# A hybrid decoder layer: the low parts of 28 weight splits made by VectorE instead of GpSimd

## The chip, the core and the metric

The kernel runs on one core of one Trainium2 chip. The core has five engines, each with its own in-order queue of instructions: TensorE (PE in the profile, with its weight loads as PEld), VectorE (DVE), ScalarE (ACT), GpSimd (POOL) and SyncE (SP, which here only starts transfers). The engines wait for one another on semaphores. The metric is the device time of one execution in microseconds (us), the median of the runs shown; lower is better.

## The reference

One decoder layer in float32 over a sequence of 2048 tokens and a model width of 1024. Two groups of heads work side by side on the same normed input, their outputs are concatenated and go through one output projection, and a SwiGLU feed-forward network follows. Cut to what matters here:

```python
hn = rms_norm(h, mix_pre_g)
proj = hn @ w_in
...
attn_out = sliding_window_attention(q, k, v, attn_sinks, rel_bias)
conv_out = conformer_conv(u, conv_dw, conv_dw_b, conv_ln_g, conv_ln_b, w_conv_pw)
mixed = jnp.concatenate([attn_out, conv_out], axis=-1) @ w_out
h = h + rms_norm(mixed, mix_post_g)
hn = rms_norm(h, ffn_pre_g)
ff = (jax.nn.silu(hn @ w_gate) * (hn @ w_up)) @ w_down
h = h + rms_norm(ff, ffn_post_g)
```

The last step of `conformer_conv` is a pointwise product with `w_conv_pw` (512 x 512) with nothing between it and the lower half of `w_out`. The two matrices can therefore be multiplied with each other once, ahead of the data.

## The kernel before

**Products in three parts.** TensorE multiplies in a reduced format (fp32r). To keep the precision of float32, each operand is split into a high part, which is the value rounded to fp32r, and a low part, raw − high, and a product is made of three matmuls: high·high, high·low and low·high (`three`). For the weights the split is made in `split_w`: ScalarE copies the raw tile into the high half (line 133), then the subtraction raw − high makes the low half. The subtraction runs either on GpSimd (`ptt`, line 135 in the trace) or on VectorE (`vtt`, which goes through the wrapper `dve` and is seen as line 85). A tile of 128 x 512 is split at a time. If a place in DRAM is given (`low`), the low half is also stored there (line 137), so that later token blocks load it (line 132) instead of making it again. `weight` loads a raw tile of two blocks and splits both.

**Stages.** The 2048 tokens are worked in four blocks of 512, t = 0 to 3:

- A0 to A3: the input projection, 14 units of 24 matmuls for each block (`mm@A` in the profile). The low parts of the weights of the first six units of block 0 are made on GpSimd, the others on VectorE.
- B0 to B3: attention of a block, in steps for each 128 queries. TensorE makes the scores (`tr@B<-kz,ql@A`), VectorE masks them (`COPY_PREDICATED`, line 457), adds the bias and takes the maximum (line 460), and prepares the shift (`sm@B`); ScalarE takes the exponentials (line 479); VectorE sums, takes the reciprocal and scales the probabilities (`p@B<-p@B,sm@B`); TensorE transposes them (line 501), ScalarE copies them out (line 502), GpSimd masks a copy (`AFFINE_SELECT`, line 504), and TensorE multiplies with the values.
- C0 to C3: the convolution over time, 480 instructions `fc@C` on VectorE (taps), followed by the normalisation over channels. The taps are put behind other work by a lower priority and, in `dve`, by an order tie to the last other VectorE instruction.
- J (`stage_join`): the product of `w_conv_pw` with the lower half of `w_out`, made once. Four raw tiles of `w_out` give eight splits (the right operands, in buffers `mid` and `chl`), two raw tiles of `w_conv_pw` give four (the left operands, in `yt`); the raw tiles lie in `wx` and `mb`. The result goes through `ct@J` and `fa@J` to DRAM as `w_join`.
- W0 to W3 (`stage_w`): the output projection of a block with norm and residual. Only W0 makes low parts of its weights (eight raw tiles, 16 splits, the first half of them of `w_out` and the second of `w_join`) and stores them in `lo_out`; W1 to W3 load them.
- H, F and G: the feed-forward network (gate and up, then down), in which VectorE makes the low parts of its operands as well (`w@F<-chl@F,w@F`).

**What sets the order.** The stages are generators on lanes that are advanced by credits: J runs on a lane beside A2 and A3, W0 beside A3 and the attention of block 2, so that their few instructions lie between those of the projection. Within that, the order of each engine's queue is not written out by hand: the tile framework places the instructions of each engine by priorities and by a simulated time line of the whole program. A change of one instruction's engine can therefore change the order of others, on all engines. Dependencies through tiles become semaphore waits.

**Buffers.** All tiles of a name share a fixed number of buffers: 6 for `w`, 2 for `raw`, 1 for `wx`, 2 for `mb`, 4 for `mid`, 5 for `chl`, 1 for `yt`. The banks of PSUM are 3 for `tr`, 4 for `mm` and 1 for `ct`. A load into a buffer waits for the last reader of what lay there.

Of the kernel before, what the change touches and what calls it, by code (L numbers as in the profile page):

```python
# [12 lines left out]
F32 = mybir.dt.float32  # L13
# [12 lines left out]
P = 128  # L26
# [11 lines left out]
def layer_kernel(ctx, tc, x, xT, cols, rows, sinks, relb, onehot, w_in, w_pw, w_out, w_gate, w_up, w_down, out):  # L38
    nc = tc.nc
# [7 lines left out]
    lab = ["X0"]  # L47
# [7 lines left out]
    def t_(tag, shape, dt=F32):  # L55
        return sb.tile(list(shape), dt, tag=tag, name=nm(tag), bufs=BUFS[tag])

    def f4(tag, shape=(P, D)):
        return t_(tag, shape)

    def f2(tag, shape=(P, T)):
        return t_(tag, shape)

    def hl(tag):
        return t_(tag, (P, 2, T), F32R)
# [63 lines left out]
    def split_w(raw, tag, low=None, made=False, on_pool=True):  # L129
        w = tag if not isinstance(tag, str) else hl(tag)  # L130
        if made:
            nc.sync.dma_start(w[:, 1].bitcast(F32), low)
        act(w[:, 0], raw, AF.Copy)  # L133
        if not made:
            (ptt if on_pool else vtt)(w[:, 1], raw, w[:, 0].bitcast(F32), ALU.subtract)
            if low is not None:
                (nc.gpsimd if on_pool else nc.sync).dma_start(low, w[:, 1].bitcast(F32))
        return w

    def weight(src, low, made, raw=None, on_pool=True):  # L140
        if raw is None:
            raw = t_("raw", (P, 2, T))
            nc.sync.dma_start(raw, src)
        return [split_w(raw[:, n], "w", low[n], made, on_pool) for n in range(2)]
# [43 lines left out]
    def three(o, pairs, first=True, last=True):  # L188
        n = 3 * len(pairs)
        i = 0  # L190
        for (sh, sl), (mh, ml) in pairs:
            for a, b in ((sh, mh), (sh, ml), (sl, mh)):
                mat(o, a, b, start=first and i == 0, stop=last and i == n - 1)
                i += 1

    lo_in = dr.tile([2 * KC - 2, 2, P, T], F32, name="lo_in")
    lo_out = dr.tile([2, KC, P, T], F32, name="lo_out")
# [425 lines left out]
    def spare_tile():  # L623
        if not spare:
            spare.append(t_("mb", (P, 2, T)))
        return spare[0]

    def stage_join():
        lab[0] = "J0"
        srcs = [w_out[4 + k].rearrange("p (a b) -> p a b", a=2) for k in range(4)]  # L630
        srcs += [w_pw[2 * m : 2 * m + 2].rearrange("m p t -> p m t") for m in range(2)]
        raws = {}

        def load(i):
            if i < len(srcs):
                lab[0] = "J0"
                raws[i] = spare_tile() if i % 2 else f4("wx", (P, 2, T))
                nc.sync.dma_start(raws[i], srcs[i])

        load(0)  # L640
        load(1)
        yield JL
        right = []
        for k in range(4):
            for n in range(2):
                lab[0] = "J0"
                right.append(split_w(raws[k][:, n], "mid" if k < 2 else "chl"))
            yield JS
            load(k + 2)
            yield JS  # L650
        for mp in range(2):
            lab[0] = "J0"
            pair_ = t_("yt", (P, 2, 2, T), F32R)
            left = [split_w(raws[4 + mp][:, m], pair_[:, m]).rearrange("p a (k c) -> p a k c", c=P) for m in range(2)]
            yield 2
            for m in range(2):
                for n in range(2):
                    lab[0] = "J0"
                    o = ct()
                    three(o, [((left[m][:, 0, k], left[m][:, 1, k]), (right[2 * k + n][:, 0], right[2 * k + n][:, 1])) for k in range(4)])  # L660
                    z = f2("fa")
                    act(z, o, AF.Copy, scale=0.5)
                    nc.scalar.dma_start(w_join[2 * mp + m, :, n * T : (n + 1) * T], z)
                    yield 4
                    lab[0] = "J0"
# [37 lines left out]
    def block_half(acc, units, n, first, L, bank_of, s0=0):  # L703
        cs = slice(n * T, (n + 1) * T)
        for i in range(len(acc)):
            s = i + s0
            lab[0] = L
            o = bank_of()
            three(o, [((a[s // 4][:, 0, ss(s)], a[s // 4][:, 1, ss(s)]), (w[:, 0], w[:, 1])) for a, w in units])
            if first:  # L710
                act(acc[i][:, cs], o, AF.Copy)
            else:
                vtt(acc[i][:, cs], acc[i][:, cs], o, ALU.add)
            yield 0.65 * len(units)

    def load_gb(row):
        gb = []
        for n in range(2):
            t = f2("gb")
            nc.sync.dma_start(t, rows[row, n * T : (n + 1) * T].partition_broadcast(P))  # L720
            gb.append(t)
        return gb
# [6 lines left out]
    def stage_w(w, spill, G, atag, htag, mtag, bank_of, norm=None):  # L729
        L = f"W{w}"  # L730
        lab[0] = L
        acc = [f4(atag) for _ in range(4)]

        def acts(gi, ms=None):
            aa = []
            for m in ms or load(gi):
                a = hl(htag)
                act(a[:, 0], m, AF.Copy)
                vtt(a[:, 1], m, a[:, 0].bitcast(F32), ALU.subtract)
                aa.append([a])  # L740
            return aa

        stage = spare_tile() if w == 1 else None

        def load(gi):
            ms = []
            for c in range(G * gi, G * gi + G):
                ms.append(stage[:, c % 2] if w == 1 else f2(mtag))
                nc.sync.dma_start(ms[-1], mixT[c, :, w * T : (w + 1) * T])
            return ms  # L750

        first = load(0)
        gb = load_gb(0) if w > 1 else None
        if w != 1:
            yield 5.0 if w == 0 else 8.0
            lab[0] = L
        nxt = acts(0, first)
        for gi in range(KC // G):
            aa = nxt
            for n in range(2):  # L760
                lab[0] = L
                if n == 0 and gi + 1 < KC // G:
                    if w < 2 and G * gi + G == 4:
                        ld.until(f"C{w}")
                        lab[0] = L
                    rows_next = load(gi + 1)
                if n == 1 and gi + 1 < KC // G:
                    nxt = acts(gi + 1, rows_next)
                src = w_out[2 * gi : 2 * gi + 2] if gi < 2 else w_join[2 * gi - 4 : 2 * gi - 2]
                ws = weight(src[:, :, n * T : (n + 1) * T].rearrange("c p t -> p c t"),  # L770
                            lo_out[n, 2 * gi : 2 * gi + 2], w > 0)
                yield from block_half(acc, list(zip(aa, ws)), n, gi == 0, L, bank_of)
        tail = norm_w(w, spill, acc, mtag, gb)
        if norm:
            norm(tail)
        else:
            yield from tail
# [627 lines left out]

    lb.add("X", stage_x(), lambda: "x1" in started)
    lw.add("W0", stage_w(0, True, 2, "x", "hl", "fa", mm), lambda: "A3" in started and "J" in ld.done)
    TGA = [["hl"] * 8, ["mid"] * 4 + ["chl"] * 4, ["hl"] * 8, ["mid"] * 4 + ["hl"] * 4]
    xa = {}
# [4 lines left out]
    for t in range(NT):  # L1414
        lc.add(f"T{t}", stage_taps(t))
    ld.add("J", stage_join(), lambda: "A2" in started)
    for t in range(2):
        ld.add(f"C{t}", stage_tail(t), lambda t=t: since(lc, f"T{t}", CS))
# [40 lines left out]
    for n, off in (("B11", 0), ("B21", 4)):  # L1459
        lh.add(n + ".0", stage_h_plain(ws, ops, n, off), lambda: since(lw, "W0", NH))  # L1460
    run(stage_w(1, True, 2, "mid", "hl", "at", mm, norm=lambda g: lh.add("N1", g)))
    lc.hold = lambda: "S0" not in lh.done
    lh.add("S0", stage_h_sums(ws, ops), lambda: f"P0.{PRE_S0}" in started and "B3" in lb.done)
# [6 lines left out]
    ws, ops = (2, 3), {}  # L1470
    lw.add("C2", stage_tail(2))
    lw.add("W2", stage_w(2, True, 2, "mid", "ql", "at", tr))
    lw.add("C3", stage_tail(3), lambda: since(lc, "T3", CS))
    lw.add("W3", stage_w(3, True, 2, "mid", "ql", "at", tr, norm=lambda g: lw.add("N3", g)))
# [72 lines left out]
```

## Time and profile before

| | before |
|---|---|
| runs, us | 1981.5, 1977.93, 1981.22 |
| median, us | 1981.22 |
| profiled execution, us | 1986.73 |
| its span, us | 1984.7 |
| mean granted clock of TensorE in it | 0.992 |

The profile is of one execution, and its times count from the start of the span. An instruction is named by line, engine, operation, and by the tiles that it writes and reads (`out<-in`), without their numbers; `x` counts instructions. In the timelines instructions of one kind that follow each other are joined in one row, with the time of the row; what stands in brackets is the idle time of that engine just before, and the instruction (or transfer) whose end released it. A granted clock of 1.00 is full speed of TensorE. The joining lies at about 185 to 300 us of the span, the making of low parts in W0 at about 330 to 443 us, the down-projection of the first half begins near 1000 us.

### The profile page before, as it was taken

The page shows a single profiled execution, that of the slowest core. Times are in us where ns is not written, and L with a number is a line of the kernel's source. Part 1 is how long each engine was busy: PE and PEld are TensorE (multiplying, and loading weights), DVE is VectorE, ACT ScalarE, POOL GpSimd, SP SyncE. Part 2 cuts the span into 40 slices and gives each one's busy share as a digit, 9 for nine tenths or more (in the row PEclk, how much of TensorE's full clock was granted, in tenths as well). Part 3 has the DMA queues.
Part 4 walks back from the last instruction along what each step waited for, and adds up shares of the span by engine and source line. Part 5 has one row for each costly group of instructions (what it writes and reads, how often), then busy time and mean ns, then how long its engine had stood idle before and what let it go on. Part 6 is the DMA issues. An engine that isn't in the chain of part 4 may idle for free.

```text
span 1984.7 us, 26851 instructions
## 1 busy us (share of the span) xinstructions
PE 1937.4 (98%) x8730; PEld 1545.6 (78%) x8730; DVE 1493.7 (75%) x2679; ACT 969.5 (49%) x1910; POOL 335.2 (17%) x395
## 2 busy tenths in 40 slices
PE   9999999999999999989999999999999999999998
PEld 7877667677768878768878878777888888888886
DVE  5998989697793899888748995688766665455557
ACT  5455334546576633333345446477544433345443
POOL 6001212331120300000000011005423332311000
PEclk9999999999999999999999999999999999999999
DMA  8886646568758676686577778679745442366654
GB/s 313 275 308 224 203 149 186 181 193 305 270 166 303 224 252 223 230 275 233 193 241 252 226 270 276 215 291 345 265 142 176 170 153 91 136 224 202 212 190 155
DMA packets 229181, 443.56 MB, mean 223 GB/s; under 512 B 22920, under 2 KB 48688, under 8 KB 229040
## 3 DMA queue, kind: packets, MB, share of 16 engines
q1 hardware_dynamic: 207408, 406.19, 61.0%
q10 hardware_dynamic: 19392, 28.32, 3.9%
q0 software_dynamic: 2240, 7.34, 0.9%
q8 instruction: 68, 1.11, 0.2%
q14 instruction: 73, 0.60, 0.1%
HBM read 320.64 MB, written 121.12 MB: 223 GB/s over the span
## 4 chain that ended last, share of the span: by engine, by line
PE 77%; DVE 8%; DMA 8%; ACT 3%; issue 2%; POOL 1%; SPq 0%; ACTq 0%; DVEq 0%; POOLq 0%
PE mm@F L108 36%; PE mm@G L108 16%; PE mm@A L108 12%; PE mm@W L108 4%; PE tr@W L108 3%; PE tr@B L108 3%; DVE fc@C L85 3%; PE ct@J L108 1%; DMA raw@A<-w_in 1%; DVE mid@W L85 1%; DMA at@W<-mixT 1%; DMA gb@F<-keeps 1%; DMA mids<-fa@F 1%; DVE w@F L85 1%; DMA mixT<-fc@C 1%
## 5 line engine op out<-in xcount | busy, mean ns | idle before, releaser
L85 DVE SCALAR_TENSOR_TENSOR fc@C<-glu@C,colt,fc@C 128x512 f32<-128x512 f32 x480 | 365.9, 778 | 2.2
L108 PE MATMUL mm@F<-hl@H,w@F 128*128 128x512 f32 x1056 | 257.6, 392 | 3.5 <-ACT mm@F L983 3.5
L108 PEld LDWEIGHTS mm@F<-hl@H,w@F 128*128 128x128 f32 x1056 | 198.7, 189 | 48.4 <-ACT mm@F L983 4.8
L108 PE MATMUL mm@G<-hl@G,hl@G 128*128 128x512 f32 x924 | 226.0, 395 | 6.6 <-ACT mm@G L1249 2.2
L108 PE MATMUL mm@A<-hl@A,w@A 128*128 128x512 f32 x840 | 209.3, 399 | 2.1 <-DVE hl@A L85 1.1
L108 PEld LDWEIGHTS mm@G<-hl@G,hl@G 128*128 128x128 f32 x924 | 172.3, 189 | 45.5 <-ACT mm@G L1249 2.6
L108 PE MATMUL mm@G<-w@G,hl@G 128*128 128x512 f32 x876 | 199.5, 389 | 0.0
L829 ACT ACTIVATE w@F<-chl@F 128x512 fp32r<-128x512 f32 x220 | 134.7, 624 | 126.4 <-PE mm@F L108 119.3
L108 PEld LDWEIGHTS mm@G<-w@G,hl@G 128*128 128x128 f32 x876 | 164.4, 188 | 34.1
L108 PEld LDWEIGHTS mm@A<-hl@A,w@A 128*128 128x128 f32 x840 | 156.8, 190 | 40.6 <-issue 3.6
L85 DVE TENSOR_TENSOR w@F<-chl@F,w@F 128x512 fp32r<-128x512 f32 x198 | 143.3, 728 | 36.9 <-ACT w@F L829 36.4
L108 PE MATMUL mm@F<-ql@H,w@F 128*128 128x512 f32 x528 | 131.3, 392 | 7.2 <-ACT mm@F L1071 3.7
L108 PE MATMUL mm@F<-mid@H,w@F 128*128 128x512 f32 x528 | 131.3, 391 | 2.8 <-ACT fa@F L1092 2.6
L108 PE MATMUL mm@F<-p@H,w@F 128*128 128x512 f32 x528 | 131.2, 394 | 0.0
L108 PE MATMUL mm@F<-x@H,w@F 128*128 128x512 f32 x528 | 127.5, 390 | 0.0
L108 PEld LDWEIGHTS mm@F<-ql@H,w@F 128*128 128x128 f32 x528 | 98.6, 188 | 28.6 <-ACT mm@F L1071 4.6
L108 PEld LDWEIGHTS mm@F<-mid@H,w@F 128*128 128x128 f32 x528 | 98.6, 188 | 24.9 <-ACT fa@F L1092 3.5
L108 PEld LDWEIGHTS mm@F<-p@H,w@F 128*128 128x128 f32 x528 | 100.7, 191 | 21.6 <-ACT at@F L1085 0.3
L108 PEld LDWEIGHTS mm@F<-x@H,w@F 128*128 128x128 f32 x528 | 98.6, 188 | 21.3 <-DVE sm@B L460 0.8
L133 ACT ACTIVATE w@A<-raw@A 128x512 fp32r<-128x512 f32 x110 | 67.4, 626 | 77.4 <-PE mm@A L108 42.9
L108 PE MATMUL mm@W<-w@W,hl@W 128*128 128x512 f32 x384 | 103.2, 408 | 1.6 <-ACT fa@A L355 1.6
L85 DVE TENSOR_TENSOR w@G<-raw@G,w@G 128x512 fp32r<-128x512 f32 x73 | 51.5, 705 | 67.7 <-ACT w@G L829 66.7
(308 smaller groups left out, 3313.9 us busy)
## 6 DMA issues: line engine op xcount, KB each, us to landing
mids<-fa@F SPq DMA_DIRECT2D x154, 256.0 KB, 2.8
raw@A<-w_in SPq DMA_DIRECT2D x55, 512.0 KB, 4.7
w@A<-lo_in SPq DMA_DIRECT2D x84, 256.0 KB, 3.7
fc@G<-mids SPq DMA_DIRECT2D x77, 256.0 KB, 3.3
fa@G<-mids SPq DMA_DIRECT2D x75, 256.0 KB, 5.0
w@W<-lo_out SPq DMA_DIRECT2D x48, 256.0 KB, 4.1
chl@F<-w_gate SPq DMA_DIRECT2D x22, 512.0 KB, 4.2
raw@F<-w_gate SPq DMA_DIRECT2D x22, 512.0 KB, 3.7
```

What stands on the lines that cost most here:

```text
L85: r = op(*args, **kw)
L108: r = nc.tensor.matmul(*args, **kw)
L133: act(w[:, 0], raw, AF.Copy)
L829: act(w[:, 0], x, AF.Copy)
```

## The change

Four lines. `split_w` has an argument `on_pool`, true by default, that picks the engine of the subtraction. The change passes `on_pool=False` at the two calls in `stage_join` (12 subtractions of 128 x 512) and in `stage_w` (16 in W0; the later blocks make none). The store of a low part, which used to go with the engine of the subtraction, is kept on GpSimd's queue for the W stages.

```diff
         if not made:
             (ptt if on_pool else vtt)(w[:, 1], raw, w[:, 0].bitcast(F32), ALU.subtract)
             if low is not None:
-                (nc.gpsimd if on_pool else nc.sync).dma_start(low, w[:, 1].bitcast(F32))
+                (nc.gpsimd if on_pool or lab[0][0] == "W" else nc.sync).dma_start(low, w[:, 1].bitcast(F32))
         return w
...
-                right.append(split_w(raws[k][:, n], "mid" if k < 2 else "chl"))
+                right.append(split_w(raws[k][:, n], "mid" if k < 2 else "chl", on_pool=False))
...
-            left = [split_w(raws[4 + mp][:, m], pair_[:, m]).rearrange("p a (k c) -> p a k c", c=P) for m in range(2)]
+            left = [split_w(raws[4 + mp][:, m], pair_[:, m], on_pool=False).rearrange("p a (k c) -> p a k c", c=P) for m in range(2)]
...
                 ws = weight(src[:, :, n * T : (n + 1) * T].rearrange("c p t -> p c t"),
-                            lo_out[n, 2 * gi : 2 * gi + 2], w > 0)
+                            lo_out[n, 2 * gi : 2 * gi + 2], w > 0, on_pool=False)
```

In the built program 28 instructions of line 135 leave GpSimd's queue and stand as subtractions of line 85 in VectorE's; the 16 stores of `lo_out` (line 137) stay on GpSimd's queue and now wait for VectorE. Counted from the start, VectorE's queue is the same up to the row that the trace shows at 192 us. From there to the beginning of the down-projection the order of the queues of all engines differs in places, and behind it it is the same again.

## The prediction

> **What bounds the kernel now.** I read the page first: busy times and the chain that ended last.
>
> ```profile
> span 1984.7 us, 26851 instructions
> PE 1937.4 (98%) x8730; PEld 1545.6 (78%) x8730; DVE 1493.7 (75%) x2679; ACT 969.5 (49%) x1910; POOL 335.2 (17%) x395
> PE 77%; DVE 8%; DMA 8%; ACT 3%; issue 2%; POOL 1%; SPq 0%; ACTq 0%; DVEq 0%; POOLq 0%
> ```
>
> TensorE (PE) bounds the whole: 1984.7 − 1937.4 = 47 us is all that it doesn't work. The change gives it no less to do, so it can gain only where PE stands still or runs at a lower clock beside the 28 subtractions that move. The next view is the busy time in stretches of 20 us over the two places (start and end, length, then busy time and count of PE, weight load, DVE, ACT, POOL, then clock, DMA share, GB/s).
>
> ```profile
> 180.00:200.00 20.00, 19.84 (x99) 15.01 (x98) 15.37 (x32) 11.03 (x32) 8.78 (x7) 1.00 0.79 287
> 200.00:220.00 20.00, 17.77 (x87) 12.01 (x83) 20.00 (x22) 8.76 (x17) 11.71 (x8) 1.00 0.73 249
> 220.00:240.00 20.00, 17.96 (x79) 13.97 (x80) 19.75 (x53) 7.24 (x24) 0.00 (x0) 0.83 0.47 151
> 360.00:380.00 20.00, 18.04 (x93) 13.97 (x90) 15.54 (x45) 19.89 (x57) 7.12 (x9) 1.00 0.51 162
> 380.00:400.00 20.00, 20.00 (x70) 10.96 (x69) 11.99 (x27) 6.41 (x11) 3.07 (x4) 1.00 0.57 176
> ```
>
> In the joining (about 185 to 225 us) DVE is full, PE falls to 17.8 of 20, and the clock drops after it. In the first output projection (332 to 442 us) DVE has room and the clock is full. The timeline of PE between 203 and 233 us shows what it waits for (start, time, instruction and count; in brackets the idle time ahead and its releaser), and two windows of 10 us show the clock.
>
> ```profile
> 205.10 0.66 PE L501 MATMUL tr@B<-ident,p@B 128*128 128x128 f32 x4 [1.12 <-DVE p@B L85]
> 206.87 0.63 PE L501 MATMUL tr@B<-ident,p@B 128*128 128x128 f32 x4 [1.11 <-DVE p@B L85]
> ...
> 215.58 4.42 PE L108 MATMUL mm@A<-hl@A,w@A 128*128 128x512 f32 x18
> ...
> 225.76 1.86 PE L108 MATMUL tr@B<-kz,ql@A 64*128 64x256 f32 x12 [2.04 <-DVE sm@B L460]
> 227.55 5.76 PE L108 MATMUL mm@A<-hl@A,w@A 128*128 128x512 f32 x14
> ```
>
> ```profile
> 220.00:230.00 10.00, 7.96 (x33) 6.12 (x34) 9.86 (x26) 1.68 (x3) 0.00 (x0) 0.78 0.55 186
> 230.00:240.00 10.00, 10.00 (x48) 7.86 (x47) 9.89 (x28) 5.56 (x21) 0.00 (x0) 0.88 0.40 117
> ```
>
> Three PE gaps, 1.12 + 1.11 + 2.04 = 4.3 us, all end on DVE. Behind the third the clock falls: 10 × (1 − 0.78) + 10 × (1 − 0.88) = 3.4 us lost (matmuls take 5.76/14 = 0.41 us against 4.42/18 = 0.25 us). So 7.7 us hang on DVE's lateness there.
>
> **Why DVE is late.** The timeline of DVE, then that of POOL, over the same stretch:
>
> ```profile
> 162.83 1.28 DVE L85 TENSOR_TENSOR p@B<-p@B,sm@B 128x512 f32<-128x512 f32 x2
> 173.52 1.88 DVE L85 TENSOR_TENSOR hl@A<-x@A,hl@A 128x512 fp32r<-128x512 f32 x3
> ...
> 193.11 1.25 DVE L85 SCALAR_TENSOR_TENSOR sm@B<-sm@B,nsnk 128x8 f32<-128x8 f32 x1
> 200.55 2.82 DVE L85 SCALAR_TENSOR_TENSOR fc@C<-glu@C,colt,fc@C 128x512 f32<-128x512 f32 x2
> 203.28 3.44 DVE L85 TENSOR_TENSOR p@B<-p@B,sm@B 128x512 f32<-128x512 f32 x2
> 206.65 10.18 DVE L85 SCALAR_TENSOR_TENSOR fc@C<-glu@C,colt,fc@C 128x512 f32<-128x512 f32 x11
> 217.36 4.05 DVE L85 SCALAR_TENSOR_TENSOR fc@C<-glu@C,colt,fc@C 128x512 f32<-128x512 f32 x6
> 223.66 0.74 DVE L457 COPY_PREDICATED tr@B<-upper,tr@B 128x256 f32<-128x256 int8 x2
> ```
>
> ```profile
> 187.84 3.54 POOL L135 TENSOR_TENSOR mid@J<-wx@J,mid@J 128x512 fp32r<-128x512 f32 x2 [0.65 <-ACT mid@J L133]
> 202.78 3.40 POOL L135 TENSOR_TENSOR chl@J<-mb@J,chl@J 128x512 fp32r<-128x512 f32 x2
> 207.45 3.46 POOL L135 TENSOR_TENSOR yt@J<-wx@J,yt@J 128x512 fp32r<-128x512 f32 x2 [1.27 <-ACT yt@J L133]
> ```
>
> DVE instructions that read two operands stretch where POOL's subtractions run: the two p@B multiplies take 3.44 us at 203 against 1.28 us at 163, two conv taps 2.82 us at 200 against 4.05/6 × 2 = 1.35 us at 217. POOL's own take 1.7 us each.
>
> **The change part by part: the joining.** Ten subtractions come to DVE in this stretch (eight right, two left). The same subtraction on DVE, hl@A, takes 1.88/3 = 0.63 us, so +6.2 us. What falls away, from the groups of DVE instructions of 180 to 225 us, and after it of 226 to 270 us, where POOL runs no such work (count, busy us, mean ns, idle before):
>
> ```profile
> L85 DVE SCALAR_TENSOR_TENSOR fc@C<-glu@C,colt,fc@C 128x512 f32<-128x512 f32 x35 | 30.1, 898 | 0.2
> L85 DVE TENSOR_TENSOR p@B<-p@B,sm@B 128x512 f32<-128x512 f32 x2 | 3.4, 1760 | 0.0
> ...
> L85 DVE SCALAR_TENSOR_TENSOR fc@C<-glu@C,colt,fc@C 128x512 f32<-128x512 f32 x38 | 27.7, 754 | 0.4
> L85 DVE TENSOR_TENSOR p@B<-p@B,sm@B 128x512 f32<-128x512 f32 x4 | 2.6, 680 | 0.0
> ```
>
> 35 × (0.898 − 0.754) + 2 × (1.76 − 0.68) = 7.2 us. DVE's total thus stays about level (−1 us); what counts is the order. In the built program of the changed kernel the eight right subtractions stand ahead of the p@B multiplies, with one tap fewer; the two multiplies end, counted from 192.2 us in undisturbed durations, at about 204.7 and 205.3 us. PE has 14 projection matmuls more ahead of the transposes that read them, 14 × 0.25 = 3.5 us of cover: it comes to them at about 207. Both first gaps go: −2.2 us.
>
> Next late is the bank of the scores, which the copy of 223.66 and four reductions free. Between the multiplies and that copy stand 16 taps (19 before), two subtractions, the rest as before: 16 × 0.67 + 2 × 0.63 + 1.7 = 13.7 us, so the copy starts near 219 and the banks are free near 222. PE has 18 matmuls more ahead of its next transposes into them (+4.5 us, less the 2.2 us it gained) and asks for them near 226. Slack 4 us: the third gap goes (−2.0), and the clock with it (−3.4). The bounds: nothing, if raws come late (SyncE's loads of wx and mb now wait for DVE's reads instead of POOL's, some 3 us later for the first); −7.7 with all. I take −7.7, as 4 us of slack stand against these 3.
>
> **The first output projection.** Sixteen subtractions leave POOL; their DMAs stay on its queue.
>
> ```profile
> L135 POOL TENSOR_TENSOR w@W<-raw@W,w@W x16: 1262/1296/2571, 331.5 to 440.6; 128x512 fp32r<-128x512 f32 x16
>   ACT w@W L133: 46.0, 8
> L137 POOL DMA_DIRECT2D lo_out<-w@W x16: 539/557/592, 334.4 to 442.4; - x16
> PE mm@W L108 <- ACT fa@A L355: 1.6, 1, 1.6
> PE tr@B L108 <- DVE sm@B L460: 0.8, 2, 0.6
> ```
>
> The last two rows are two of the three waits of PE between 350 and 460 us: none is for these subtractions, so making them 1.30 − 0.63 us faster gains nothing. The price is on DVE: 16 × 0.63 = 10 us more work (in 380 to 400 us it was busy 12 of 20), and a new wait. POOL stood 46.0 us in eight waits for ACT's high parts; on DVE everything behind would stand too: taps, the scale and sum of the softmax, p@B multiplies, the copies that free banks, and PE behind these. How long DVE stands, the nearest row tells, the same kind of split of the FFN:
>
> ```profile
> L85 DVE TENSOR_TENSOR w@F<-chl@F,w@F 128x512 fp32r<-128x512 f32 x198 | 143.3, 728 | 36.9 <-ACT w@F L829 36.4
> 382.49 0.69 DVE L85 TENSOR_TENSOR hl@W<-fa@W,hl@W 128x512 fp32r<-128x512 f32 x1 [3.48 <-ACT hl@W L738]
> ```
>
> 36.4/198 = 0.18 us each, 16 of them 2.9 us; at the other end the single 3.48 us of hl@W. Of DVE's waits PE saw little (0.8 us). I take +1.0 of PE time; bounds 0 and the slower rival's 16. POOL's stores now wait for DVE, with the attention's masks behind them; the kernel's POOL is 17% busy, and I take 0.
>
> **Given back and reordered.** The order differs on all engines until the down-projection (near 1000 us). PE comes 7.7 us earlier to later waits, such as the 1.6 us above; I give back 1.4 us, half of 1.6 and of the joining's own 1.1:
>
> ```profile
> PE ct@J L108 <- ACT fa@J L662: 1.1, 1, 1.1
> 576.97 4.61 PE L108 MATMUL mm@F<-hl@H,w@F 128*128 128x512 f32 x12 [1.92 <-ACT mm@F L983]
> 844.53 1.65 PE L108 MATMUL mm@F<-ql@H,w@F 128*128 128x512 f32 x6 [2.39 <-ACT mm@F L1071]
> ```
>
> Gaps like that of 576.97 (1.9 us, with 12 × (0.384 − 0.246) = 1.7 us of low clock behind it) can come or go by this reordering: ±4 us, at 0 in the sum.
>
> **Sum:** −7.7 + 1.0 + 1.4 = −5.3 us. The profiled execution lasted 1986.73 us (span 1984.7), so it would be 1981.4; that execution lies 5.5 us over the median of the runs, 1981.22, from which the same difference gives **1976 us**.
>
> **The rivals.** *The clock's loss doesn't hang on the gap.* For it: at 844.53 a gap of 2.39 us is followed by full speed (1.65/6 = 0.275 us). Against it: 225.76 and 576.97. Then the low stretch falls elsewhere and only gaps go: −4.3 + 2.4 = −1.9, 1979.3 us. The Trainium skill has such a rule in "TensorE: Matmul & The Clock Gate", "Why this matters for your kernels": idle gaps of PE up to about 3 us cost no clock; by it this rival's sum would hold. The trace disagrees at 2.04 and 1.92 us.
>
> *DVE's queue stalls on ACT in the output projection (slower).* Between 360 and 380 us ACT is full (19.89 of 20) and its high parts lie behind the softmax's exponentials; a subtraction ahead of a score's scale or copy holds the next head. Each place with a stall of 3.5 us gives a PE gap of about 1.9 and 3.4 us of clock: 5.3. From two places on it eats the gain; three give 16 − 7.7 = +8: 1989 us. Against it: PE never waited on DVE over 0.6 us there.
>
> *The reordering helps too.* One stretch like that at 576.97 goes as well: 1972 us.
>
> **How the numbers follow.** About 0.2%, 4 us, can be told from no change here. The forecast has 0.44 (its own range 1971 to 1979; 0.06 of it within 0.2%), the clock rival 0.12 (within), the slower rival 0.34 (0.02 within), the helping order 0.10. So faster 0.48, same 0.20, slower 0.32. The range, 1969 to 1988, leaves out the best orders and the stalls at three places or more.
>
> **What would show it.** Right: no two p@B multiplies over 1.5 us beside the joining, no PE waits for p@B and sm@B near 205 and 226 us, clock 1.00 from 220 to 240; subtractions of 0.63 us on DVE. Wrong: a PE wait for sm@B or p@B between 330 and 450 us with DVE idle for ACT's w@W ahead of it; a gap moved to another place before 1000 us; or clock below 1.00 after 205 without a gap.

## The result, and the profile after

The changed kernel takes 1970.68 us (median of 6 runs, 1968.0 to 1973.53) against 1981.36 us (6 runs, 1977.93 to 1988.69): a ratio of 0.9941, 95% interval 0.9927 to 0.9955, or 10.7 us less. The forecast was 1976 us in a range of 1969 to 1988. The profiled execution of the changed kernel lasted 1968.13 us, 2.6 under its median, and that of before 1986.73, 5.4 over its own; the two profiles therefore differ by 18.6 us where the medians differ by 10.7, and stage times below are read with that in mind.

Page of the changed kernel: span, busy times, and the chain that ended last.

```profile
span 1966.4 us, 26845 instructions
PE 1929.6 (98%) x8730; PEld 1542.5 (78%) x8730; DVE 1490.1 (76%) x2707; ACT 974.5 (50%) x1914; POOL 289.4 (15%) x367
PE 84%; DMA 6%; DVE 5%; ACT 2%; issue 2%; POOL 1%; SPq 0%; ACTq 0%; DVEq 0%; POOLq 0%
```

DVE does 28 instructions more and is not busier (1490.1 us against 1493.7): the subtractions cost what the stretching had cost. Its share of the chain fell from 8% to 5%. The stretches of 20 us in the changed kernel:

```profile
200.00:220.00 20.00, 20.00 (x97) 14.21 (x96) 20.00 (x35) 9.05 (x17) 1.72 (x2) 1.00 0.83 297
220.00:240.00 20.00, 20.00 (x102) 15.72 (x102) 19.79 (x57) 7.74 (x25) 0.00 (x0) 1.00 0.55 173
```

TensorE now works all of both, at full clock, and DVE is as full as before. DVE's timeline there, then TensorE's:

```profile
193.70 0.68 DVE L85 TENSOR_TENSOR mid@J<-wx@J,mid@J 128x512 fp32r<-128x512 f32 x1
...
204.54 1.28 DVE L85 TENSOR_TENSOR p@B<-p@B,sm@B 128x512 f32<-128x512 f32 x2
...
219.53 0.75 DVE L457 COPY_PREDICATED tr@B<-upper,tr@B 128x256 f32<-128x256 int8 x2
...
222.50 1.41 DVE L85 SCALAR_TENSOR_TENSOR fc@C<-glu@C,colt,fc@C 128x512 f32<-128x512 f32 x2
```

```profile
207.53 1.03 PE L501 MATMUL tr@B<-ident,p@B 128*128 128x128 f32 x8
...
225.68 0.97 PE L108 MATMUL tr@B<-kz,ql@A 64*128 64x256 f32 x12
```

The two p@B multiplies take 1.28 us (3.44 before) and end at 205.8; TensorE reads them at 207.5 without a wait. The copy that frees the score banks starts at 219.5, the last reduction ends at 222.5, and TensorE comes at 225.7.

In the first output projection, DVE's groups from 310 to 450 us (count, busy us, mean ns, idle before and its releaser):

```profile
L85 DVE SCALAR_TENSOR_TENSOR fc@C<-glu@C,colt,fc@C 128x512 f32<-128x512 f32 x77 | 57.0, 753 | 0.4
...
L85 DVE TENSOR_TENSOR w@W<-raw@W,w@W 128x512 fp32r<-128x512 f32 x16 | 10.9, 686 | 2.2 <-ACT w@W L133 2.1
```

The 16 subtractions take 0.69 us each, DVE stands 2.1 us in all for ScalarE's high parts, and the taps beside them are back to 753 ns (846 in the same stretch of the kernel before). TensorE has one wait left there:

```profile
PE mm@W L108 <- ACT hl@W L738: 1.0, 1, 1.0
```

### The profile page after: what moved, and what is told of

It is laid out like the page before. It is cut to its first block, busy times and chain, and to the rows that moved or that the text cites. A ratio compares the mean times of both kernels' runs of the same rounds, so it can differ in the third digit from the quotient of the medians.

```text
span 1966.4 us, 26845 instructions
## 1 busy us (share of the span) xinstructions
PE 1929.6 (98%) x8730; PEld 1542.5 (78%) x8730; DVE 1490.1 (76%) x2707; ACT 974.5 (50%) x1914; POOL 289.4 (15%) x367
## 4 chain that ended last, share of the span: by engine, by line
PE 84%; DMA 6%; DVE 5%; ACT 2%; issue 2%; POOL 1%; SPq 0%; ACTq 0%; DVEq 0%; POOLq 0%
PE mm@F L108 36%; PE mm@G L108 18%; PE mm@A L108 15%; PE mm@W L108 5%; PE tr@W L108 4%; PE tr@B L108 4%; PE ct@J L108 1%; PE tr@B L501 1%; DVE w@F L85 1%; DMA at@W<-mixT 1%; DVE fc@C L85 1%; DMA td<-fc@G 1%; DVE mid@W L85 1%; DMA mixT<-fc@C 1%; DMA at@W<-x 1%
## 5 line engine op out<-in xcount | busy, mean ns | idle before, releaser
L85 DVE SCALAR_TENSOR_TENSOR fc@C<-glu@C,colt,fc@C 128x512 f32<-128x512 f32 x480 | 354.2, 752 | 2.1
```

What stands on the lines that cost most here:

```text
L85: r = op(*args, **kw)
```

## The experiments

Twelve kernels were run. The table gives the ratio to the kernel before, timed beside it on the same chip, and the accounts of one profiled execution each: when the last product of the joining started (last `ct@J`), then all idle time of TensorE, the time lost to the clock (over windows of 10 us, 10 x (1 − granted clock)), and the rest of the time up to TensorE's last matmul (work at full clock, with the extra spacing between matmuls of different shape).

| kernel | ratio (95%) | last `ct@J`, us | idle | clock | rest |
|---|---|---|---|---|---|
| before | 1 | 309.5 | 35.8 | 13.6 | 1925.5 |
| changed | 0.9941 (0.9927 to 0.9955) | 299.1 | 25.7 | 10.2 | 1921.0 |
| join_only | 0.9978 (0.9959 to 0.9996) | 299.3 | 36.2 | 8.5 | 1922.2 |
| w0_only | 1.0030 (1.0012 to 1.0049) | 309.2 | 39.8 | 17.0 | 1925.8 |
| join_both | 0.9954 (0.9936 to 0.9972) | 306.1 | 29.0 | 12.0 | 1920.6 |
| join_memset | 0.9993 (0.9980 to 1.0006) | 301.2 | 31.2 | 15.3 | 1925.2 |
| memset_w0 | 0.9944 (0.9924 to 0.9964) | 302.8 | 28.9 | 13.7 | 1922.4 |
| before_rw18 | 1.0016 (0.9996 to 1.0036) | 309.7 | 35.4 | 13.6 | 1925.3 |
| after_rw18 | 0.9939 (0.9911 to 0.9967) | 299.1 | 26.4 | 11.9 | 1918.8 |
| store_sync | 0.9932 (0.9906 to 0.9959) | 300.0 | 30.5 | 13.6 | 1918.6 |
| memset_order | 0.9986 (0.9966 to 1.0007) | 300.8 | 31.5 | 6.8 | 1925.9 |
| w0_order | 1.0032 (1.0015 to 1.0050) | 311.5 | 39.7 | 20.4 | 1925.8 |
| after_late | 0.9921 (0.9895 to 0.9946) | 298.4 | 26.8 | 1.7 | 1921.4 |
| all_dve | 1.0006 (0.9988 to 1.0025) | 306.2 | 29.4 | 13.6 | 1924.5 |

Two things have to be known to compare these accounts. First, the executions differ before the joining begins. At 187 us, where TensorE has had the same queue in all kernels but `all_dve`, it is 0.6 us earlier in the kernel before than in the changed one, and later by 0.3 us in `join_only`, 1.8 in `w0_only`, 1.3 in `join_both`, 0.4 in `join_memset`, 2.0 in `memset_w0`, 2.3 in `before_rw18` and 1.5 in `w0_order`; the others lie within 0.9 us. Counted from there, the last `ct@J` of the kernel before starts 11.0 us later than that of the changed kernel. Second, the clock's loss in the table is that of one execution. For every run the span and the mean granted clock are known. Span × (1 − clock) is on average 14.2 us in the kernel before (79 runs on three chips), 15.1 us in the changed one (6 runs) and 10.8 to 17.9 us in the others. What remains, span × clock, is 1967.2 us before and 1953.7 us after. So over the runs the change gains idle time and spacing, and no gain of clock is seen. This remainder is called the time without the clock's loss below.

**The two halves alone.** Against the changed kernel, `join_only` undoes the edit in `stage_w` and that of the store; `w0_only` undoes the two in `stage_join`. First `join_only`, then `w0_only`:

```diff
-                            lo_out[n, 2 * gi : 2 * gi + 2], w > 0, on_pool=False)
+                            lo_out[n, 2 * gi : 2 * gi + 2], w > 0)
```

```diff
-                right.append(split_w(raws[k][:, n], "mid" if k < 2 else "chl", on_pool=False))
+                right.append(split_w(raws[k][:, n], "mid" if k < 2 else "chl"))
...
-            left = [split_w(raws[4 + mp][:, m], pair_[:, m], on_pool=False).rearrange("p a (k c) -> p a k c", c=P) for m in range(2)]
+            left = [split_w(raws[4 + mp][:, m], pair_[:, m]).rearrange("p a (k c) -> p a k c", c=P) for m in range(2)]
```

> Only the 12 low parts of the joining move to VectorE; those of the first output projection stay on GpSimd. Theory (VectorE late in the joining because GpSimd's subtractions stretch its instructions): the three TensorE waits near 204, 206 and 224 us are gone and the clock is 1.00 there, so 7.7 us less than before in that stretch; whole time 6 to 9 us under the kernel before. Rival (most of the 10.7 us comes from the first output projection and the reordering behind it): 2 to 4 us under it.

> Only the 16 low parts of the first output projection move to VectorE; the joining is as before. Theory: the three waits and the low clock near 225 us stay as before, and what the output projection gives is small, 0 to 3 us under the kernel before (its waits of 0.64 and 1.56 us may go). Rival: 6 to 9 us under it.

`join_only` is 4.4 us faster (0.0022 of 1983), `w0_only` 6 us slower; together they give 11.7. Neither theory has that: the halves do not add. The clock isn't the reason: the time without its loss is 5.5 us under the kernel before in `join_only`, 4.8 us over it in `w0_only`, and 13.5 us under it with both. In the stretch of the joining the first theory holds: `join_only` starts its last `ct@J` at 299.3 us and the changed kernel at 299.1, `w0_only` at 309.2 and the kernel before at 309.5. Counted from 187 us, though, `w0_only` needs 8.3 us more than the changed kernel and the kernel before 11.0. What makes the whole times differ comes later. TensorE's waits between 310 and 575 us (total, times, longest), in `join_only` first, then in `w0_only`:

```profile
PE ct@C L559 <- DMA fc@C<-y_scr: 3.0, 1, 3.0
PE mm@F L108 <- ACT mm@F L983: 1.9, 1, 1.9
```

```profile
PE mm@W L108 <- DVE ql@A L85: 2.5, 1, 2.5
PE mm@W L108 <- ACT x@W L711: 2.1, 1, 2.1
```

Each has waits of 2 to 3 us that the changed kernel has not, at places that belong to no edited line. `w0_only` also shows the joining's third wait once more, but not the low clock behind it; TensorE's row, and the windows of 10 us around it:

```profile
228.28 1.28 PE L108 MATMUL tr@B<-kz,ql@A 64*128 64x256 f32 x12 [2.04 <-DVE sm@B L460]
```

```profile
220.00:230.00 10.00, 7.92 (x40) 5.81 (x40) 9.96 (x25) 2.78 (x5) 0.00 (x0) 1.00 0.73 234
230.00:240.00 10.00, 10.00 (x52) 7.98 (x52) 9.79 (x25) 4.08 (x20) 0.00 (x0) 1.00 0.26 82
```

The same 2.04 us as in the kernel before cost 3.4 us of clock there and none here.

**The contention alone, order held.** In `join_both` GpSimd makes the joining's subtractions again, for nobody.

```diff
-            (ptt if on_pool else vtt)(w[:, 1], raw, w[:, 0].bitcast(F32), ALU.subtract)
+            (ptt if on_pool else vtt)(w[:, 1], raw, w[:, 0].bitcast(F32), ALU.subtract); lab[0][0] == "J" and ptt(junk.bitcast(F32), raw, w[:, 0].bitcast(F32), ALU.subtract)
```

> The changed kernel, in which GpSimd makes the 12 subtractions of the joining a second time, into a scratch tile that nobody reads; the queues of TensorE, VectorE, ScalarE and SyncE keep the changed kernel's order row by row. Theory (contention): VectorE's instructions beside them stretch again, the p@B multiplies end 4 to 8 us later than at 205.8 us, TensorE waits there again and the clock falls; 4 to 9 us over the changed kernel. Rival (the new order is what helps, with 14 and 18 matmuls more ahead of the waiting transposes): under 1.5 us over it.

The queues of the four other engines are row for row those of the changed kernel. The timelines of GpSimd, of DVE and of TensorE, and the window behind its wait:

```profile
202.53 3.13 POOL L135 TENSOR_TENSOR junk<-wx@J,chl@J 128x512 f32<-128x512 f32 x2 [0.98 <-ACT chl@J L133]
205.74 3.33 POOL L135 TENSOR_TENSOR junk<-mb@J,chl@J 128x512 f32<-128x512 f32 x2
```

```profile
206.14 1.78 DVE L85 TENSOR_TENSOR chl@J<-wx@J,chl@J 128x512 fp32r<-128x512 f32 x1
...
212.07 1.28 DVE L85 TENSOR_TENSOR p@B<-p@B,sm@B 128x512 f32<-128x512 f32 x2
```

```profile
212.80 1.97 PE L501 MATMUL tr@B<-ident,p@B 128*128 128x128 f32 x8 [2.75 <-DVE p@B L85]
```

```profile
210.00:220.00 10.00, 7.25 (x30) 6.22 (x30) 10.00 (x13) 4.37 (x8) 5.89 (x4) 0.83 0.76 273
```

A subtraction on DVE takes 1.78 us instead of 0.68 beside GpSimd's, the p@B multiplies end 7.5 us later (213.3 against 205.8), TensorE waits 2.75 us and loses 1.7 us of clock. Of these 7.5 us, 1.3 were there before GpSimd's first subtraction, from a wait of 2.4 us near 30 us of this execution and the low clock behind it. The last `ct@J` starts 7.0 us later; its rows in the changed kernel and in `join_both` (count, duration, first and last start):

```profile
L108 PE MATMUL ct@J<-chl@J,yt@J x48: 388/389/477, 236.2 to 299.1; 128*128 128x512 f32 x48
```

```profile
L108 PE MATMUL ct@J<-chl@J,yt@J x48: 388/389/478, 243.1 to 306.1; 128*128 128x512 f32 x48
```

This is the contention shown by itself: less the 1.3 us of the start, 5.7 of the joining's 11.0 us. Of the whole time 2.6 us remain by the ratios (0.0013), between the rival's 1.5 and the theory's 4, and in intervals that overlap; what the contention costs in the whole time is therefore not shown.

**The contention taken away, order of before.** `join_memset` has GpSimd write zeros in place of the joining's low parts.

```diff
-            (ptt if on_pool else vtt)(w[:, 1], raw, w[:, 0].bitcast(F32), ALU.subtract)
+            nc.gpsimd.memset(w[:, 1].bitcast(F32), 0.0) if lab[0][0] == "J" else (ptt if on_pool else vtt)(w[:, 1], raw, w[:, 0].bitcast(F32), ALU.subtract)
```

> The kernel before, with GpSimd writing zeros in place of the 12 subtractions of the joining, so the products lack the low parts there; the p@B multiplies and their transposes keep the order of before. Theory (contention): with no GpSimd reads beside them, VectorE's p@B multiplies take 1.3 us again and end about 7 us earlier (near 200 us), the three waits go, 6 to 9 us under the kernel before. Rival (order): the waits stay, under 3 us.

The joining came out as the theory had it: p@B as below, none of the three waits, last `ct@J` at 301.2 us. The whole time did not: 0.9993. Counted from 187 us, its joining is 9.3 us shorter than that of the kernel before, and 6.6 us shorter than the same joining in `w0_only` and `before_rw18`, which lost no clock in it: in the order of before too, most of the joining's gain comes with GpSimd's reads taken away. And a gain of 7 to 9 us by 310 us of the span can be lost again. The p@B row, and TensorE's largest wait between 310 and 575 us:

```profile
200.94 1.28 DVE L85 TENSOR_TENSOR p@B<-p@B,sm@B 128x512 f32<-128x512 f32 x2
```

```profile
PE mm@W L108 <- ACT fa@A L355: 3.6, 1, 3.6
```

**The output projection on top of that.** `memset_w0` is the changed kernel with those zeros in the joining.

```diff
-            (ptt if on_pool else vtt)(w[:, 1], raw, w[:, 0].bitcast(F32), ALU.subtract)
+            nc.gpsimd.memset(w[:, 1].bitcast(F32), 0.0) if lab[0][0] == "J" else (ptt if on_pool else vtt)(w[:, 1], raw, w[:, 0].bitcast(F32), ALU.subtract)
```

> The kernel with zeros written by GpSimd in place of the joining's subtractions (its products lack the low parts there), and the low parts of the first output projection on VectorE as in the change. Theory now (the joining gives 10 us by 310 us of the span however GpSimd's reads are taken away; whether that is kept is settled by the order of the queues behind it, which the output projection's low parts change): between 0 and 12 us under the kernel before. If the low parts of the output projection help by themselves once TensorE comes early: 5 to 8 us under join_memset's ratio, that is 0.995 to 0.997. If they harm by themselves, as w0_only suggests: 1.002 or more.

0.9944, so 0.0049 (10 us) under `join_memset`. With the joining's waits gone, the 16 subtractions on DVE gain 7 us (`join_only` to changed) or 10 us (`join_memset` to `memset_w0`); with the waits there they lose 6 us. "They help once TensorE comes early" fits all three pairs. What makes it so is the next question.

**Order as the cause: one place of ScalarE's queue.** In the kernel before, in `w0_only` and in `join_memset` the copy `fa@A<-mm@A` (line 355), which empties a bank, stands behind the eight exponentials of a softmax, and TensorE waits there 1.6, 2.1 and 3.6 us (in `w0_only` for another bank just ahead of it). In the changed kernel it stands ahead of them. Three kernels set that order by hand; `memset_order` and `w0_order` put it ahead, `after_late` (with the arguments of `after_first` exchanged) behind. `held` collects the exponentials as they are written.

```diff
-                act(th, og, AF.Tanh, scale=0.5)
+                r = act(th, og, AF.Tanh, scale=0.5); [after_first(r, e) for e in held[-16:-8] if uid[0] == 599]
...
-                act(pr[:, h], pr[:, h], AF.Exp, bias=negm[:, h : h + 1], accum_out=den[:, h : h + 1])
+                held.append(act(pr[:, h], pr[:, h], AF.Exp, bias=negm[:, h : h + 1], accum_out=den[:, h : h + 1]))
```

> join_memset (zeros in place of the joining's low parts) with one order set by hand on ScalarE: the copy fa@A that empties a bank of the projection (uid 599) stands ahead of the eight exponentials of the softmax, not behind them. Theory (the joining's gain was given back at that copy, where TensorE waited 3.6 us and then ran at half clock for 3.4 us): no wait over 1.2 us there, 4 to 8 us under join_memset, that is a ratio to before of 0.995 to 0.997. Rival (the low parts of the output projection on VectorE are what keeps the gain): as join_memset, 0.999.

> w0_only (low parts of the output projection alone on VectorE) with the same hand-set order on ScalarE. Theory (order): the wait of 2.05 us behind the exponentials and the low clock of 360 to 410 us go, 3 to 6 us under w0_only: ratio to before 0.999 to 1.002. Rival (stalls of VectorE by the low parts themselves): as w0_only, 1.003.

> The changed kernel with the opposite order set by hand: the copy fa@A (uid 599) behind the eight exponentials. Theory (order): TensorE waits 1.5 to 3.5 us for that bank again, and with the clock 3 to 7 us over the changed kernel: ratio to before 0.9955 to 0.9975. Rival (the order of ScalarE at this place doesn't matter): as the changed kernel, 0.994.

None of the three came out as the theory had it. `after_late`, which was to lose 3 to 7 us, lost nothing: its ratio is the lowest of all (0.9921, not separable from the changed kernel), and its time without the clock's loss, 1954.1 us, is that of the changed kernel (1953.7); TensorE didn't wait for the copy there. In `w0_order` the wait of 2.1 us behind the exponentials went (0.6 us are left), and the time is that of `w0_only`. `memset_order` stays within noise of `join_memset`. The intervals of the last two still reach into the theory's ranges; that of `after_late` doesn't. TensorE's waits in `memset_order` from 310 to 575 us tell why a single place decides nothing:

```profile
PE mm@W L108 <- ACT fa@A L355: 2.0, 1, 2.0
PE tr@B L501 <- DVE p@B L85: 1.8, 1, 1.8
PE tr@B L108 <- DVE sm@B L460: 1.3, 2, 0.9
```

The wait for the copy fell by 1.6 us, and the softmax that was put back came late by 1.8 and 1.3.

**A shuffle of the FFN, and the stores.** One pacing constant changed in both kernels, and (second) the stores of the changed kernel issued from SyncE.

```diff
-    RC0, RC1, RC2, RC3, RW0, RW, RB, LC = 0.7, 1.1, 0.4, 0.9, 1.7, 1.25, 0.8, 100
+    RC0, RC1, RC2, RC3, RW0, RW, RB, LC = 0.7, 1.1, 0.4, 0.9, 1.8, 1.25, 0.8, 100
```

```diff
-                (nc.gpsimd if on_pool or lab[0][0] == "W" else nc.sync).dma_start(low, w[:, 1].bitcast(F32))
+                (nc.gpsimd if on_pool else nc.sync).dma_start(low, w[:, 1].bitcast(F32))
```

> The kernel before with one pacing constant changed (RW0 1.7 to 1.8, the rate of the lane of the first output projection); TensorE's queue keeps its order to row 2313 (the FFN), so joining and output projection are as before, the FFN's order is shuffled. If the order alone is worth several us: 0.4% or more from the kernel before, either way. If order is a small matter: within 0.15%.

> The changed kernel with the same pacing constant changed; TensorE's queue keeps its order to row 2150. If the change's gain lies before the FFN, this stands 8 to 12 us under before_rw18; if it hangs on the FFN's order, the distance is under 5 or over 15 us.

> The changed kernel with the 16 stores of low parts issued from SyncE instead of GpSimd. The joining is the same, the order differs from the first output projection on. If stores behind VectorE on GpSimd's queue cost nothing, as the prediction took, the time is that of the changed kernel but for the order: within 5 us of it. If they hold up the attention's masks: 3 us or more under it. Waiting stores on SyncE's queue may hold up loads: then over it by 5 us or more.

The shuffle moves the kernel before by +0.16% and the changed one by −0.02%, both within their intervals. The distance between the two is 0.0077 (15 us; 13.7 by the medians), at the edge of what was expected of either case; with intervals of 0.002 and 0.003 it is not separable from the 11 us of the unshuffled pair. Sign and rough size of the gain survive another order of the FFN; more this pair doesn't settle. `store_sync` is 0.0009 under the changed kernel: stores behind DVE on GpSimd's queue cost nothing that can be measured, with intervals of some 5 us either way.

**All of GpSimd's subtractions moved.**

```diff
-        hs = weight(w_in[u].rearrange("p (a b) -> p a b", a=2), lo_in[u], made, raw, u < TAPS0)
+        hs = weight(w_in[u].rearrange("p (a b) -> p a b", a=2), lo_in[u], made, raw, False)
```

> The changed kernel with the low parts of the first six units of the input projection on VectorE too, which leaves GpSimd no such subtraction at all (their stores go to SyncE). If contention at the start costs as in the joining: VectorE loses 12 x 0.63 us of room and gains about as much, and TensorE, which waited 0.6 us for these, gains 1 to 3 us: 0.992 to 0.994. If VectorE is the late one there: over the changed kernel by 2 us or more.

1.0006: the whole gain is gone. A part of it is clock: these runs lose 17.9 us to it on average, and without that loss the kernel is 2.4 us under the kernel before and 11.1 over the changed one. The joining is as in the changed kernel to its first `ct@J` (234.8 us, 234.4), then a wait of 2.7 us for a softmax copy and 1.7 us of clock between 260 and 320 us bring the last one to 306.2. Where the other microseconds go was not followed up. Moving more of the same kind of work isn't better by itself.

## Why the prediction was right, point by point

**The joining.** "Both first gaps go", "the third gap goes", "and the clock with it": as forecast, and every instant within 0.6 us: the multiplies' end 205.3 (205.8 measured), the copy near 219 (219.5), banks free near 222 (222.5), TensorE near 226 (225.7). The slack was 3.2 us instead of 4. By the last `ct@J` the changed kernel is 10.4 us ahead where the terms said 7.7: idle −5.0 (mostly the three waits, and the 1.1 us at `ct@J`), clock −3.4, and −2.0 in the rest. That contention is the cause is shown twice: `join_both` brings 5.7 us back with GpSimd's reads alone, and `join_memset` gains 6.6 to 9.3 us without them in the order of before.

The clock's −3.4 us is not a fixed price of the third gap. Four profiled kernels have the joining of before. In two of them (before, `w0_order`) 3.4 us of clock went in it, and their joining takes 11.0 and 10.9 us more than that of the changed kernel; in the other two (`w0_only`, `before_rw18`) the same gap of 2.04 or 2.05 us cost no clock, and it takes 8.3 us more. Over the runs the changed kernel doesn't lose less to the clock than the kernel before. This term of the sum came true in the profile, and partly by luck.

**The first output projection, +1.0.** The forecast wait of DVE was 2.9 us, measured 2.1, and TensorE saw none of it in the changed kernel: 0 instead of +1.0. The sum put 10 us more work on DVE and took nothing off; the taps beside it fell from 64.3 to 57.0 us (78 and 77 of them). Alone, in `w0_only`, this half costs 6 us, at places the forecast didn't name.

**"I give back 1.4 us", and the reordering "±4 us, at 0 in the sum".** These are the steps that were mis-sized, beside the joining. The 1.1 and 1.6 us waits went rather than came nearer. Behind the joining the two profiles differ by another 7.6 us (18.0 in all to TensorE's end), but not all of it is order. At 862 us of the kernel before, from where on the queues of TensorE, VectorE, ScalarE and GpSimd are row for row the same in both, the changed kernel is 13.3 us ahead. The other 4.7 us arise where the order is the same, most of them at a wait near 875 us (3.5 us before, 2.15 after) with low clock behind it in the kernel before alone. So −10.4 us in the joining and −2.9 us from there to 862 us stand against the forecast's −7.7 and +2.4. That is 8 us more than forecast in these two executions, which lie 7.9 us further apart than the medians do. With the 4.7 us taken off, some 3 of the 8 us are left to the executions and 5 to the terms, an estimate; which term holds these 5 us, between 5.3 and 10.7, the runs don't show.

That the total fell into the range is in part luck. The sum adds two halves, −6.3 with the give-back and +1.0; measured alone they are −4.4 and +6, and together −11.7. The mechanism of the joining was right; that the halves can be added was not.

Over the whole span the rest fell by 4.5 us, 2.0 of them in the joining, and idle time by 10.1, 5.0 of them there. A part of the rest may come from the order of matmuls. TensorE alternates scores (64 x 256) and projections (128 x 512); in the kernel before around 500 us:

```profile
503.80 0.49 PE L108 MATMUL mm@W<-w@W,hl@W 128*128 128x512 f32 x1
504.23 0.38 PE L108 MATMUL tr@B<-kz,ql@A 64*128 64x256 f32 x1
504.54 0.51 PE L108 MATMUL mm@W<-w@W,hl@W 128*128 128x512 f32 x1
```

A pair takes 0.74 us so, against 0.23 (one projection matmul in a row of its kind, start to start) and, where twelve scores follow each other (0.97 us), 0.08: 0.43 us lost at each pair. Counted over the trace up to the last attention matmul, the kind of matmul (scores, products with values, transposes, others) changes 262 times before and 249 times after, 245 in `join_only`, 281 in `w0_only`: 13 changes, or some 6.5 pairs, would be 2.8 us. This estimate doesn't carry over: `w0_only` has 19 changes more than the kernel before and a rest only 0.3 us longer. So the share is not shown.

**The rivals.** That the clock's loss doesn't hang on the gap was given 0.12, and it was half right: the 2.04 us gap kept its low clock in the kernel before and had none in `w0_only`. The traces show what decides it. In every profile the stretches at half clock are 3.41 us long or a multiple of that, and within a profile their starts lie whole multiples of 3.41 us apart. Cut into windows at these places, the gap of the kernel before (223.72 to 225.76 us) lies nearly whole in one window, and the next two run at half clock. That of `w0_only` (226.24 to 228.28) is split over two windows, 1.18 and 0.90 us. So is the 2.39 us gap ahead of 844.53, which the prediction held against its own clock term. The windows of the three, in this order, with the columns of the stretches above (the first busy time is TensorE's, the clock is the third value from the end):

```profile
222.25:225.67 3.42, 1.48 (x7) 0.89 (x5) 3.42 (x13) 0.63 (x1) 0.00 (x0) 1.00 0.67 226
225.67:229.08 3.41, 3.32 (x16) 2.73 (x17) 3.28 (x8) 0.42 (x1) 0.00 (x0) 0.50 0.34 139
229.08:232.49 3.41, 3.41 (x10) 2.64 (x9) 3.39 (x7) 0.00 (x0) 0.00 (x0) 0.50 0.20 77
```

```profile
224.01:227.42 3.41, 2.23 (x10) 1.50 (x8) 3.41 (x8) 0.63 (x1) 0.00 (x0) 1.00 0.61 243
227.42:230.83 3.41, 2.51 (x18) 1.99 (x19) 3.31 (x13) 0.42 (x1) 0.00 (x0) 1.00 0.60 212
```

```profile
840.07:843.48 3.41, 2.07 (x10) 1.37 (x8) 1.53 (x3) 0.00 (x0) 0.00 (x0) 1.00 0.56 197
843.48:846.89 3.41, 2.24 (x9) 1.54 (x10) 3.41 (x7) 2.20 (x4) 0.00 (x0) 1.00 0.92 299
```

Over the 14 profiles, the first 20 us left out, each of the 51 windows at full clock in which TensorE stood for 1.9 us or more is followed by one at half clock, none of the 194 with 0.4 to 1.4 us is, and 18 of the 66 in between are. The rule of the Trainium skill, "TensorE: Matmul & The Clock Gate", section "What's actually happening", is that the clock is judged in windows of about 3.4 us that run on by themselves. The traces agree, with their 3.41 us. So whether a gap of 2 us costs clock depends on where in a window it falls, which differed between these executions.

The slower rival, DVE's queue stalling on ScalarE, didn't occur: DVE stood 0 to 3.3 us in all for these high parts in the nine kernels that have the subtractions there, 1.4 us in `w0_only`, which is slower for other reasons. That the new order helps too was given 0.10. Its 1972 us lie nearer to the measured 1970.7 than the forecast's 1976, and in the profile the 1.92 us wait near 577 us shrank to 0.5, as it said; it is not shown how much of the gain that is. Two of the signs of being wrong appeared as well: a new wait of 2.9 us near 664 us (for `fa@F`, with 3.4 us of clock behind it), and a clock below 1.00 without a gap behind 488 us (5.1 us).

**What stays open.** Why the output projection's half gains 7 to 10 us behind a joining without waits and loses 6 us behind one with them. The runs show idle time, clock and shape changes all moving with the order of the queues, and that one named place of ScalarE's queue isn't the cause; the clock's loss isn't either, as the time without it shows the same signs. Orders could not be held fixed for this half, as they were in `join_both`, so contention and order are not told apart there.

## What to carry to other kernels

Where two-operand work on VectorE is on the way to TensorE, the same work on GpSimd is not free: compare the duration of one VectorE instruction beside GpSimd's and away from it (3.44 against 1.28 us here) before calling GpSimd idle capacity. In a kernel whose queues are ordered by a scheduler, an edit is judged as a whole: halves of this one gave −4 and +6 us and together −12, and a fix of one wait moved it to the next. What the clock took is read from all runs and not from one profile: in single profiles it was 1.7 to 20.4 us here, in the averages of the kernels 10.8 to 17.9. A theory of contention can be tested cleanly by adding the load where nobody reads it, if the other queues keep their order.

## What the runs showed of the hardware

TensorE's clock can also fall where the profile's rows, whose matmul ends are modelled, show no idle gap. In the changed kernel this happened in a stretch of alternating shapes (scores and projections, 483 to 494 us). Windows of the changed kernel, then of `after_late`, where TensorE is as busy:

```profile
480.00:490.00 10.00, 10.00 (x36) 5.96 (x34) 6.60 (x10) 7.66 (x11) 2.12 (x3) 0.93 1.05 386
490.00:500.00 10.00, 10.00 (x23) 6.66 (x24) 7.64 (x19) 2.95 (x6) 0.00 (x0) 0.56 0.71 269
```

```profile
480.00:490.00 10.00, 10.00 (x35) 5.76 (x33) 6.78 (x10) 7.56 (x11) 2.89 (x6) 1.00 1.04 399
490.00:500.00 10.00, 10.00 (x51) 7.74 (x51) 9.34 (x30) 4.73 (x9) 0.00 (x0) 1.00 0.87 314
```

5.1 us were lost in the one and none in the other, with TensorE busy throughout. The shapes alternate in `after_late` too (483 to 491 us), so alternation alone doesn't decide it. Over the 14 profiles, 11 windows of 3.41 us with less than 0.4 us of idle time were followed by half clock. All 11 have only 8 to 11 matmuls starting in them (15 is usual), but of 99 such windows 88 were followed by full clock. What tells them apart stays open. Over the 14 profiles the loss of clock lies between 1.7 and 20.4 us, as much as the effect that was studied.
